# A hybrid decoder block in one kernel: the second feed-forward matmul adds products up in PSUM and scales its results, and the first stage loads x first and ada_w in groups

## The chip, the cores and the metric

The kernel runs on one core of one Trainium2 chip. The metric is the device time of one execution in microseconds (us). Every array lies in HBM at the start and at the end. The engines named below are PE (TensorE), DVE (VectorE), ACT (ScalarE), POOL (GpSimd) and SP (SyncE, which here only issues DMA transfers).

## What is computed

One layer of a decoder for a sequence of 1024 tokens with 1024 features, all in float32. The mixing half of the layer is not touched by the change, so it is left out here:

```python
c_act = jax.nn.silu(c)
mod = (c_act @ ada_w + ada_b)[:, None, :]
sh1, sc1, gt1, sh2, sc2, gt2 = jnp.split(mod, 6, axis=-1)

h = rms_norm(x, norm_mix_g) * (1.0 + sc1) + sh1
p = h @ w_in
...
h = rms_norm(x, norm_ffn_g) * (1.0 + sc2) + sh2
x = x + gt2 * (jnp.square(jax.nn.relu(h @ ffn_w1)) @ ffn_w2)
return rms_norm(x, final_g)
```

`ada_w` is 1024 x 6144, `w_in` is 1024 wide on its contracted side, `ffn_w1` is 1024 x 4096 and `ffn_w2` 4096 x 1024.

## The kernel before, in words

**Precision.** A float32 factor is split in two parts, a rounded high part and the rest, by `split` (L72 an ACT cast, L73 a DVE subtraction). One product of two 128-row tiles is then three matmuls into the same PSUM tile, `mm3` (L112, L113, L114): high with high, high with low, low with high.

**Order.** A scheduler sets the order on each engine from the order in which the code issues its instructions and from a model of their cost; an engine works its queue off in that order, and an instruction that waits holds up what stands behind it. SP's queue holds nearly all loads and stores.

**First stage, `start` (L356 to L437).** The 1024 features are 8 tiles of 128 (`kt`). For each `kt`, `ada_load` fetches the 128 columns of `ada_w` for the shift and the 128 for the scale; `ada_sum` multiplies them by silu(c) and adds them up over the 8 row tiles on DVE (L270 once, L272 seven times, 128x256 each); `ada_col` has PE add over the partitions (L141) and writes the columns `sh` and `s` (L281, L282). The scaled x (L353) is transposed on PE (L338); ACT applies `sh` and `s` and writes the high part `hh` and an exact copy `ev` (L390); `hl`, the low part, is the difference on POOL (L392; for the last `kt` on DVE). `w_load` and `w_split` bring in 384 columns of one row tile of `w_in` as `raw`, `whi`, `wlo`, with two buffers each. `main` then does the matmuls for one `kt` and one half of 512 tokens: 3 column blocks times 3. The loop does half 0 of a `kt` and then half 1 of the one before. The next stage (columns of branch D, `n` and `hh` in the trace) mixes into the end.

**Second feed-forward matmul, `ffn_down` (L1455 to L1625), the last stage.** It multiplies the squared relu, transposed and stored by the stage before in the DRAM array `FA`, by `ffn_w2`. It is one level of a seven-product (Strassen-like) scheme: tokens, contracted features and output columns are each halved, and seven products of sums and differences of blocks take the place of eight. `FA` holds the seven left factors ready-made; the right factors are made here, tile by tile, by `operand`: on POOL (L1498 and L1501, differences of halves of `e` and `o`, which are even and odd row tiles of the weights), then split by ACT and DVE. The contracted side is worked through in two passes `c` of `m` = 8 tiles each; in each pass the seven products `k` run in the tuple `order`, each over 8 tiles (steps) for 4 token tiles `t`, so that one product is 8 x 4 x 3 = 96 matmuls into four PSUM banks. Two sets of four banks (`mm`, and `ch`, `ch`, `ax`, `ax`) take turns.

The gate `gt2` scales columns. Before, it is applied to the weights: in pass 0 inside `operand` (L1495, 24 tiles on DVE, 8 on POOL), and on POOL behind the loads for pass 1 (L1477, 32). `evict` takes each product out of PSUM: in pass 0 into 28 tiles of SBUF (ACT), in pass 1 by a DVE add (L1508); a list `todo` of further DVE adds from SBUF to SBUF combines the products. `lower`, `right` and `top` add x, take the squares for the final norm, and store. The evictions of the stage before, the first feed-forward matmul, are L1406.

## Time and profile before

| | us |
|---|---|
| median of 3 runs | 1723.52 (1723.36 to 1727.23) |
| the profiled execution's own time | 1722.87 |
| its span in the trace | 1721.1 |

The trace has the start and the length of every instruction on every engine in this one execution, and for a wait the instruction that ended it. PE is busy for 95% of the span. Spacing between starts of matmuls is a surer measure of PE than its busy time, because a matmul's record overlaps the next one's; the columns of the windows also give TensorE's granted clock, where 1.00 stands for its upper level of 2.4 GHz and 0.50 for the lower of 1.2 GHz. Times of day below are us from the span's start: the first stage lies at 0 to 93, `ffn_down`'s matmuls at 1372 to 1713.

### The profile page before, as it was taken

To read this page: it belongs to the slowest core of one execution; us is meant where nothing else is said; L and a number is where in the kernel's file an instruction comes from. 1 tells how busy PE (TensorE), PEld (TensorE's weight loads), DVE (VectorE), ACT (ScalarE), POOL (GpSimd) and SP (SyncE) were. 2 spreads that over 40 slices of the span, in tenths; PEclk is the share of its full clock that TensorE was granted. 3 is DMA by queue.
4 is the path that set the end of the run, shared out by engine and by line. 5 is a ranking of instruction groups with operands and counts; after the bars stand their busy time and mean duration, and the time that the engine had idled before them with its cause. 6 is when DMAs were issued, how large, how long until landed. Compare 5 with 4: busy or idle time off the path is not lost.

```text
span 1721.1 us, 22750 instructions
## 1 busy us (share of the span) xinstructions
PE 1626.4 (95%) x8083; PEld 1302.1 (76%) x8083; DVE 1066.9 (62%) x1778; ACT 657.1 (38%) x1214; POOL 688.3 (40%) x536
## 2 busy tenths in 40 slices
PE   4899999999999999999999997899999979999987
PEld 2698777777776877777888775688888757888876
DVE  5674546666539734333444659765555599889986
ACT  4522124555522112121222335544445435544443
POOL 2450223112211222222001457576665486676553
PEclk9999999999999999999999999899999989999998
DMA  8433136777666435332212544454444653563252
GB/s 251 113 99 58 57 118 195 179 187 180 151 124 193 90 112 167 110 96 56 67 44 86 187 142 123 129 184 141 153 153 153 208 189 111 185 194 104 90 180 91
DMA packets 268804, 234.68 MB, mean 136 GB/s; under 512 B 79287, under 2 KB 200362, under 8 KB 268690
## 3 DMA queue, kind: packets, MB, share of 16 engines
q1 hardware_dynamic: 260082, 224.83, 44.1%
q10 hardware_dynamic: 8464, 8.01, 1.9%
q8 instruction: 64, 1.05, 0.3%
q0 software_dynamic: 144, 0.39, 0.1%
q14 instruction: 50, 0.41, 0.1%
HBM read 172.59 MB, written 60.58 MB: 135 GB/s over the span
## 4 chain that ended last, share of the span: by engine, by line
PE 41%; DVE 7%; issue 2%; DMA 1%; POOL 1%; ACT 1%; POOLq 0%; DVEq 0%; SPq 0%; ACTq 0%
PE pmm L113 8%; PE pmm L112 8%; PE pmm L114 8%; PE pax L114 3%; PE pax L113 3%; PE pax L112 3%; PE pch L113 3%; PE pch L114 3%; PE pch L112 3%; DVE g L73 1%; DVE w L1495 1%; DMA raw<-in_ffn_w_dram 1%; DVE xx L73 1%; DMA x<-X 1%; POOL x L1535 0%
## 5 line engine op out<-in xcount | busy, mean ns | idle before, releaser
L112 PE MATMUL pmm<-hh,whi 128*128 128x512 f32 x704 | 287.0, 410 | 2.7 <-ACT hh L390 2.6
L113 PE MATMUL pmm<-hl,whi 128*128 128x512 f32 x704 | 279.5, 397 | 5.5 <-POOL hl L392 5.5
L114 PE MATMUL pmm<-hh,wlo 128*128 128x512 f32 x704 | 279.3, 397 | 3.5 <-DVE wlo L73 3.2
L73 DVE TENSOR_TENSOR wlo<-raw,whi 128x512 fp32r<-128x512 f32 (+1 forms) x140 | 107.2, 802 | 136.4 <-ACT whi L72 133.1
L114 PEld LDWEIGHTS pmm<-hh,wlo 128*128 128x128 f32 x704 | 133.5, 190 | 35.2 <-DVE wlo L73 4.9
L113 PEld LDWEIGHTS pmm<-hl,whi 128*128 128x128 f32 x704 | 134.0, 190 | 34.0 <-POOL hl L392 8.1
L112 PEld LDWEIGHTS pmm<-hh,whi 128*128 128x128 f32 x704 | 133.3, 190 | 33.7 <-ACT hh L390 4.1
L72 ACT CAST whi<-raw 128x512 fp32r<-128x512 f32 (+1 forms) x140 | 79.3, 612 | 159.6 <-PE pmm L113 106.6
L1220 POOL TENSOR_TENSOR m<-m,sig 128x512 f32<-128x512 f32 x32 | 45.1, 1409 | 130.0 <-DVE sig L1217 129.8
L84 POOL TENSOR_TENSOR raw<-raw,gt 128x1024 f32<-128x1024 f32 x16 | 38.8, 2427 | 136.5 <-DMA raw<-in_w_o_dram 131.3
L1203 ACT ACTIVATE sig<-pmm 128x512 f32<-128x512 f32 x64 | 38.1, 595 | 142.7 <-PE pmm L114 135.1
L73 DVE TENSOR_TENSOR g<-raw,g 128x512 fp32r<-128x512 f32 x75 | 79.8, 1064 | 20.1 <-ACT g L72 14.1
L72 ACT CAST g<-raw 128x512 fp32r<-128x512 f32 x75 | 46.5, 619 | 82.1 <-PE pmm L113 47.9
L73 DVE TENSOR_TENSOR g<-w,g 128x512 fp32r<-128x512 f32 x65 | 74.4, 1145 | 3.0 <-ACT g L72 2.8
L1217 DVE TENSOR_TENSOR sig<-pmm,sig 128x512 f32<-128x512 f32 x48 | 33.0, 687 | 68.6 <-PE pmm L114 68.6
L73 DVE TENSOR_TENSOR n<-xx,m 128x512 fp32r<-128x512 f32 x64 | 55.0, 865 | 28.3 <-ACT m L72 28.3
L1501 POOL TENSOR_TENSOR w<-w,w 128x512 f32<-128x512 f32 x32 | 54.4, 1705 | 44.7 <-DVE g L73 34.2
L72 ACT CAST m<-xx 128x512 fp32r<-128x512 f32 x64 | 39.3, 620 | 75.4 <-PE pch L113 27.4
L113 PE MATMUL pmm<-g,g 128*128 128x512 f32 x152 | 61.2, 402 | 6.3 <-DVE g L73 6.3
L112 PE MATMUL pmm<-n,wyh 128*128 128x512 f32 x160 | 66.3, 416 | 0.8 <-ACT n L72 0.8
L1406 DVE TENSOR_TENSOR xx<-pmm,xx 128x512 f32<-128x512 f32 x52 | 35.8, 689 | 47.4 <-PE pmm L114 43.4
L113 PE MATMUL pmm<-n,wyh 128*128 128x512 f32 x160 | 64.6, 404 | 0.0
(522 smaller groups left out, 4383.5 us busy)
## 6 DMA issues: line engine op xcount, KB each, us to landing
raw<-FA SPq DMA_DIRECT2D x56, 512.0 KB
raw<-in_w_in_dram SPq DMA_DIRECT2D x52, 512.0 KB
FA<-xx SPq DMA_DIRECT2D x80, 256.0 KB
raw<-in_ffn_w_dram SPq DMA_DIRECT2D x36, 512.0 KB
mod<-in_ada_w_dram SPq DMA_DIRECT2D x64, 256.0 KB
w<-in_ffn_w_dram SPq DMA_DIRECT2D x32, 512.0 KB
ada<-in_ada_w_dram SPq DMA_DIRECT2D x16, 512.0 KB
raw<-in_w_o_dram SPq DMA_DIRECT2D x16, 512.0 KB
```

The lines of the kernel that those rows point to most:

```text
L72: a = nc.scalar.copy(hi, src)
L73: b = (eng or nc.vector).tensor_tensor(lo, src, hi.bitcast(F32), op=ALU.subtract)
L84: nc.gpsimd.tensor_tensor(raw, raw, scale, op=ALU.mult)
L112: mm(ps, lhsT=lh, rhs=rh, start=start, stop=False)
L113: mm(ps, lhsT=lh, rhs=rl, start=False, stop=False)
L114: mm(ps, lhsT=ll, rhs=rh, start=False, stop=stop)
L1203: nc.scalar.activation(sg, pg, AF.Sigmoid)
L1217: v.tensor_tensor(m if first else sg, py[0], sg, op=ALU.mult)
L1220: nc.gpsimd.tensor_tensor(m, m, sg, op=ALU.add)
L1406: v.tensor_tensor(dst, pts[i, k], u, op=ALU.add)
L1495: eng.tensor_tensor(w[:, h], w[:, h], gt2[:, h], op=ALU.mult)
L1501: gp.tensor_tensor(src, {5: e[:, h1], 6: o[:, h1], 4: o[:, h0]}[k], src, op=ALU.subtract)
```

## The change

**In `ffn_down`.** The order of the products becomes 1, 5, 6, 3, 7, 4, 2. Products 6 and 7 go on adding in the four banks where product 1 stands, and 3 in those of product 5 (`behind`); the banks are read out after 1, 5, 3, 7, 4 and 2, each time with the running sum (`into`). In pass 0 this leaves 16 copies on ACT and 16 adds on DVE; in pass 1, 32 adds from PSUM on DVE, and the adds from SBUF to SBUF are gone but for four in pass 0. The gate scales the results: 8 tiles on DVE and 8 on POOL, and for product 2 of pass 1, whose result goes straight into x, the 8 weight tiles on POOL. x comes in earlier for the upper token tiles, and `lower` runs during the last product, together with `lower_right`.

**In `start`.** x of the first half is loaded ahead of `ada_w`; `ada_w` comes in groups of 1, 1, 2, 2, 2 tiles, where a row of a pair is 1 KB instead of 512 B, and a pair is added up by 8 DVE instructions of 128x512; `w_in` comes in pairs, so that its two buffers hold four tiles; x of the first half is scaled for its first 512 features on ACT; `hl` of half 0 is made on DVE instead of POOL.

The diff, cut to this:

```diff
-    def ada_load(self, j):
+    def ada_load(self, j, n):
...
+        w = self.ADA.tile([P, KT, 2, n * P], F32, tag=f"ada{n}", name=f"ada_{self.n}")
+        src = self.a["ada_w"][0].rearrange("(k p) f -> p k f", p=P)
+        for k in (slice(0, KT // 2), slice(KT // 2, KT)):
+            for sec in range(2):
+                c0 = sec * D + j * P
+                self.nc.sync.dma_start(w[:, k, sec], src[:, k, c0 : c0 + n * P])
...
+                if first and hf == 0:
+                    nc.scalar.activation(x[hf], x[hf], AF.Identity, scale=st[:, 3, t : t + 1])
...
-            eng = v if kt == KT - 1 else nc.gpsimd
+            eng = v if kt == KT - 1 or half == 0 else nc.gpsimd
...
             if kt == 0:
-                with self.tc.issue_after(self.last.ins):
-                    acc.append(self.ada_sum(ada[2]))
-            elif kt + 2 < KT:
-                acc.append(self.ada_sum(ada[kt + 2]))
+                add(2)
+            elif kt in (1, 2):
+                add(3, KT // 2)
+            elif kt in (3, 4):
+                if kt == 3:
+                    ada(6, 2)
+                    w_load(3)
+                add(4, KT // 2)
...
-        order = (1, 7, 5, 6, 4, 3, 2)
+        order = (1, 5, 6, 3, 7, 4, 2)
...
-            if i >= m:
-                for h in (h0, h1):
-                    gp.tensor_tensor(w[:, h], w[:, h], gt2[:, h], op=ALU.mult)
...
-            for eng, w, h in {1: ((v, e, h0), (v, e, h1)), 7: ((v, o, h1),), 5: ((gp, o, h0),)}.get(k, ()):
-                if i < m:
-                    eng.tensor_tensor(w[:, h], w[:, h], gt2[:, h], op=ALU.mult)
+            if k == 2 and i >= m:
+
+                gp.tensor_tensor(o[:, h0], o[:, h0], gt2[:, h0], op=ALU.mult)
...
+        into = {1: ("11",), 5: ("22",), 6: ("12",), 3: ("12",), 7: ("21", "22"), 4: ("21",), 2: ("11",)}
+        behind = {6: 1, 7: 6, 3: 5}
+        ends = (3, 7, 4, 2)
...
+            for j in into[k]:
+                if (j, t) in acc:
+                    a = acc[j, t]
+
+                    add(a, acc["21", t] if c == 0 and j == "22" else pt, a)
+                else:
+                    a = acc[j, t] = self.g()
+                    nc.scalar.copy(a, pt)
+            if c == 1:
+                later = {
+                    1: lambda: join(gp, t, 0, acc["11", t]),
+                    3: lambda: right(t),
+                    7: lambda: scale(gp, acc["22", t], 1),
+                    4: lambda: (lower_right(t), lower(t)),
+                }
...
+                if k in behind:
+                    pts = banks[c, behind[k]]
+                else:
+                    first = (k in (1, 2)) == (c == 0)
+                    pts = [self.ps(tag) for tag in (("mm",) * 4 if first else ("ch", "ch", "ax", "ax"))]
```

The instruction order between the first stage and `ffn_down` is the same on every engine. Three places where it differs:

SP's queue in the first stage, behind the loads of the first two tiles of `ada_w` (`ada`) and of both halves of x. Before, with `raw` a single row tile of `w_in`:

```order
L261 DMA ada_248<-in_ada_w_dram 128x8x128 x2
L365 DMA raw_251<-in_w_in_dram 128x384
L261 DMA ada_253<-in_ada_w_dram 128x8x128 x2
L365 DMA raw_256<-in_w_in_dram 128x384
L261 DMA ada_327<-in_ada_w_dram 128x8x128 x2
L261 DMA ada_390<-in_ada_w_dram 128x8x128
L365 DMA raw_330<-in_w_in_dram 128x384
```

and after the change, with two tiles to each load:

```order
L264 DMA ada_184<-in_ada_w_dram 128x4x256 x4
L374 DMA raw_189<-in_w_in_dram 128x2x384
L264 DMA ada_191<-in_ada_w_dram 128x4x256 x4
L374 DMA raw_196<-in_w_in_dram 128x2x384
L264 DMA ada_481<-in_ada_w_dram 128x4x256 x4
L374 DMA raw_486<-in_w_in_dram 128x2x384
```

What stood there as single tiles of `ada_w` and single row tiles of `w_in` in turn now comes in pairs: three loads of `ada_w`, of four transfers each, bring its tiles 2 to 7, and each has the matching pair of `w_in` behind it. `ada_481` takes over the buffer of `ada_184`, as `raw_330` took over that of `raw_251`.

DVE in the first stage, around the sums for the third tile of `ada_w` (`aacc_318` before, with `aacc_381` that of the fourth; `aacc_322` after the change is that of both). Before:

```order
L272 SCALAR_TENSOR_TENSOR aacc_318<-ada_248,cact,aacc_318 128x256
L270 TENSOR_SCALAR aacc_381<-ada_253,cact 128x256
L272 SCALAR_TENSOR_TENSOR aacc_318<-ada_248,cact,aacc_318 128x256
L272 SCALAR_TENSOR_TENSOR aacc_381<-ada_253,cact,aacc_381 128x256
L272 SCALAR_TENSOR_TENSOR aacc_318<-ada_248,cact,aacc_318 128x256
L73 TENSOR_TENSOR wlo_356<-raw_251,whi_355 128x384
L272 SCALAR_TENSOR_TENSOR aacc_318<-ada_248,cact,aacc_318 128x256
L272 SCALAR_TENSOR_TENSOR aacc_381<-ada_253,cact,aacc_381 128x256
L281 TENSOR_TENSOR sh_95<-pax_341,prmT 128x1
L282 SCALAR_TENSOR_TENSOR s_94<-pax_341,b_122,prmT 128x1
```

after the change, with `m` a tile of x and `wlo` the low part of `w_in`:

```order
L361 TENSOR_SCALAR m_181<-m_181,st_49_289 128x512
L277 SCALAR_TENSOR_TENSOR aacc_322<-ada_184,cact,aacc_322 128x512
L73 TENSOR_TENSOR wlo_355<-raw_189,whi_354 128x384
L277 SCALAR_TENSOR_TENSOR aacc_322<-ada_184,cact,aacc_322 128x512
L73 TENSOR_TENSOR wlo_355<-raw_189,whi_354 128x384
L277 SCALAR_TENSOR_TENSOR aacc_322<-ada_184,cact,aacc_322 128x512 x2
L275 TENSOR_SCALAR aacc_380<-ada_191,cact 128x512
L286 TENSOR_TENSOR sh_95<-pax_340,prmT 128x1
L287 SCALAR_TENSOR_TENSOR s_94<-pax_340,b_122,prmT 128x1
```

The sum of the fourth tile is no longer a row of its own behind the third's shift and scale (`sh`, `s`): both tiles' sums end ahead of them.

DVE where `ffn_down` begins, with `w` the tiles of `ffn_w2`, `gt` the gate, `g` and `xx` split factors. Before:

```order
L1406 TENSOR_TENSOR xx_11795<-pmm_11838,xx_11795 128x512
L73 TENSOR_TENSOR xx_11914<-raw_11873,xx_11913 128x512
L1495 TENSOR_TENSOR w_2052_11883<-w_2052_11883,gt_11866 128x512
L73 TENSOR_TENSOR xx_11916<-w_2051_11881,xx_11915 128x512
L73 TENSOR_TENSOR g_2072_11926<-w_2052_11883,g_2071_11925 128x512
L1495 TENSOR_TENSOR w_2053_11885<-w_2053_11885,gt_11866 128x512
L73 TENSOR_TENSOR g_2087_11956<-raw_11875,g_2086_11955 128x512
L1495 TENSOR_TENSOR w_2053_11885<-w_2053_11885,gt_11866 128x512
L73 TENSOR_TENSOR g_2089_11958<-w_2053_11885,g_2088_11957 128x512
L73 TENSOR_TENSOR xx_11978<-raw_11875,xx_11977 128x512
L1495 TENSOR_TENSOR w_2054_11887<-w_2054_11887,gt_11866 128x512 x2
L73 TENSOR_TENSOR g_2096_12002<-raw_11953,g_2095_12001 128x512
```

after the change, where L1425 is the eviction that was L1406:

```order
L73 TENSOR_TENSOR g_2060_11876<-raw_11831,g_2059_11875 128x512
L1425 TENSOR_TENSOR xx_11775<-pch_11761,xx_11706 128x512
L73 TENSOR_TENSOR g_2062_11878<-w_2042_11841,g_2061_11877 128x512
L73 TENSOR_TENSOR g_2077_11906<-raw_11833,g_2076_11905 128x512
L1425 TENSOR_TENSOR xx_11755<-pax_11779,xx_11755 128x512
L73 TENSOR_TENSOR g_2079_11908<-w_2043_11843,g_2078_11907 128x512
L1425 TENSOR_TENSOR xx_11753<-pmm_11796,xx_11753 128x512
L73 TENSOR_TENSOR xx_11868<-raw_11831,xx_11867 128x512
L73 TENSOR_TENSOR xx_11870<-w_2041_11839,xx_11869 128x512
L73 TENSOR_TENSOR xx_11926<-raw_11833,xx_11925 128x512
L73 TENSOR_TENSOR xx_11928<-w_2044_11845,xx_11927 128x512
L73 TENSOR_TENSOR g_2086_11948<-raw_11903,g_2085_11947 128x512
```

The multiplications by the gate are gone from between the splits, and nothing stands in their place.

## Rows read from the trace of the kernel before

**Rows 1.** The page: PE's busy tenths in 40 slices of 43 us

```profile
PE   4899999999999999999999997899999979999987
```

**Rows 2.** Windows of the first stage: each engine's busy us, clock, DMA share, GB/s

```profile
35.00:40.00 5.00, 1.54 (x5) 1.25 (x5) 2.29 (x7) 0.00 (x0) 3.41 (x1) 0.72 0.27 64
40.00:45.00 5.00, 3.70 (x15) 2.92 (x14) 2.61 (x8) 0.85 (x2) 0.00 (x0) 0.50 0.33 92
...
50.00:55.00 5.00, 5.00 (x30) 4.02 (x28) 4.96 (x13) 3.19 (x5) 2.74 (x2) 1.00 0.83 219
```

**Rows 3.** PE's waits, 0 to 90 us: total, times, longest

```profile
PE pax L141 <- DVE aacc L272: 9.7, 2, 8.4
PE pmm L113 <- POOL hl L392: 5.5, 4, 3.5
```

**Rows 4.** Timeline of DVE and SP: start, length, what, idle time before

```profile
30.74 1.68 DVE L353 TENSOR_SCALAR m<-m,st 128x512 f32<-128x512 f32 x4 [1.14 <-POOL st L350]
...
41.59 0.56 DVE L73 TENSOR_TENSOR wlo<-raw,whi 128x384 fp32r<-128x384 f32 x1 [4.30 <-ACT whi L72]
...
42.17 0.34 SPq L365 DMA_DIRECT2D raw<-in_w_in_dram  x1
...
43.71 0.16 DVE L281 TENSOR_TENSOR sh<-pax,prmT 128x1 f32<-128x1 f32 x1 [0.77 <-PE pax L141]
```

**Rows 5.** Groups of instructions by line, 0 to 90 us: busy, mean ns, idle before

```profile
L392 POOL TENSOR_TENSOR hl<-ev,hh 128x512 fp32r<-128x512 f32 x14 | 21.9, 1571 | 39.0 <-ACT ev L390 39.0
...
L392 DVE TENSOR_TENSOR hl<-ev,hh 128x512 fp32r<-128x512 f32 x2 | 1.4, 692 | 0.6 <-ACT ev L390 0.6
```

**Rows 6.** Timeline of PE at the end of the first stage

```profile
86.25 0.51 PE L112 MATMUL pmm<-n,hh 128*128 128x256 f32 x1
...
91.17 0.40 PE L113 MATMUL pmm<-hl,whi 128*128 128x512 f32 x1
```

**Rows 7.** Timeline of PE in `ffn_down`: first matmuls, first wait, later matmuls, last one

```profile
1372.38 0.39 PE L112 MATMUL pmm<-g,g 128*128 128x512 f32 x1
...
1377.17 0.50 PE L112 MATMUL pmm<-g,g 128*128 128x512 f32 x1 [2.59 <-DVE xx L1406]
...
1379.48 0.63 PE L114 MATMUL pmm<-g,g 128*128 128x512 f32 x1
1379.91 0.63 PE L112 MATMUL pmm<-g,g 128*128 128x512 f32 x1
...
1712.79 0.39 PE L114 MATMUL pax<-g,g 128*128 128x512 f32 x1
```

**Rows 8.** Windows of `ffn_down`, columns as in rows 2

```profile
1410.00:1420.00 10.00, 6.93 (x24) 5.21 (x24) 10.00 (x7) 5.55 (x11) 9.34 (x6) 0.84 0.00 0
...
1450.00:1500.00 50.00, 50.00 (x222) 41.38 (x221) 42.84 (x37) 24.61 (x44) 35.67 (x23) 1.00 0.54 177
```

**Rows 9.** PE's waits, 1340 to 1480 us: first and last of five groups

```profile
PE pch L113 <- DVE g L73: 4.8, 1, 4.8
...
PE pmm L113 <- DVE xx L73: 1.2, 1, 1.2
```

**Rows 10.** PE's waits, 1480 to 1722 us: first and last of three groups

```profile
PE pmm L113 <- DVE xx L73: 4.1, 1, 4.1
...
PE pch L113 <- DVE xx L73: 0.9, 1, 0.9
```

**Rows 11.** Groups of instructions by line, 1370 to 1450 us

```profile
L1495 DVE TENSOR_TENSOR w<-w,gt 128x512 f32<-128x512 f32 x22 | 30.3, 1402 | 0.0
...
L1495 POOL TENSOR_TENSOR w<-w,gt 128x512 f32<-128x512 f32 x8 | 13.8, 1729 | 0.0
...
L1501 POOL TENSOR_TENSOR w<-w,w 128x512 f32<-128x512 f32 x8 | 13.4, 1675 | 8.0 <-DVE g L73 4.3 <-DVE xx L73 3.7
```

**Rows 12.** Groups by line, 1480 to 1722 us

```profile
L1508 DVE TENSOR_TENSOR n<-n,m 128x512 f32<-128x512 f32 x16 | 16.1, 1024 | 0.0
...
L1527 DVE SCALAR_TENSOR_TENSOR x<-x,st,fg 128x512 f32<-128x512 f32 x12 | 8.6, 750 | 5.2 <-POOL st L1522 5.2
```

More of the change, by code (lines that the diff above doesn't have):

```diff
@@ L377, in start, with add @@
         self.new_h()
-        ada = [self.ada_load(0)]
+        raws, ws, accs = [], [], []
+        sums = []
+        ada = lambda j, n: sums.append(self.ada_sum(self.ada_load(j, n), n, accs))
         xs = [self.load_x(0)]
-        raws = [w_load(0), w_load(1)]
-        ada.append(self.ada_load(1))
+        ada(0, 1)
+        w_load(0)
+        ada(1, 1)
         xs.append(self.load_x(1))
+        ada(2, 2)
+        w_load(1)
+        ada(4, 2)
+        w_load(2)
         pts = [self.ps(t) for t in ("mm", "mm", "mm", "mm", "ch", "ch")]
+        def add(g, n=KT):
+            for _ in range(n):
+                next(sums[g], None)
         def pre(kt, half):
@@ L1525, in normed, with join @@
         def normed(tt, ch, r):
-            x = x1[tt][:, ch]
+            x = x1[tt, ch]
             v.scalar_tensor_tensor(x, x, r, fg[:, ch], op0=ALU.mult, op1=ALU.mult)
         def put(tt, ch):
-            nc.sync.dma_start(self.out[0, tt * P : tt * P + P, h1 if ch else h0], x1[tt][:, ch])
+            nc.sync.dma_start(self.out[0, tt * P : tt * P + P, h1 if ch else h0], x1[tt, ch])
+        def join(eng, tt, ch, a):
+            scale(eng, a, ch)
+            gp.tensor_tensor(x1[tt, ch], x1[tt, ch], a, op=ALU.add)
         def lower(t):
             tt = 4 + t
-            for ch in range(2):
-                gp.tensor_tensor(x1[tt][:, ch], x1[tt][:, ch], acc[4 + ch, t], op=ALU.add)
-                square(tt, ch, acc[4 + ch, t])
+            join(v, tt, 0, acc["21", t])
+            square(tt, 0, acc["21", t])
             r = root(tt)
@@ L1590, in ffn_down @@
             b_load(i, 1)
-        x1 = {}
+        banks = {}
         for s, (c, k, i) in enumerate(steps):
@@ L1604, in ffn_down @@
                     tok = slice(t * P, t * P + P)
-                    self.mm3(pts[t], ah[:, tok], al[:, tok], bh, bl, q == 0, q == m - 1)
+                    self.mm3(pts[t], ah[:, tok], al[:, tok], bh, bl, q == 0 and k not in behind, q == m - 1 and k in ends,
+                             open_=True)
                     if q == m - 1:
```

130 lines of the change are left out of this document (58 added, 72 removed).

## The prediction

> **What bounds the kernel now.** I read the page's slices first. PE is at nine tenths or more in most of them [rows 1]; the dips are slices 1 and 2 (0 to 86 us), 25 and 26 (1033 to 1119), 33 (1377 to 1420) and the last two (from 1635). At 25 and 26 no engine's order changes, so nothing there can move; the others lie in the two stages that the change touches. That leaves two places.
>
> The first is 35 to 50 us. PE does 1.54 of 5 us, then 3.70, and the 3.70 at the lower clock, 0.50 [rows 2]. The waits name what PE stands for: 9.7 us on the sums of `ada_w` (one wait of 8.4), and 5.5 us on `hl` from POOL [rows 3]. DVE's timeline shows why the sum is late. DVE itself stands idle for 4.30 us until 41.59, because the next row in its queue splits a tile of `w_in`, and the rest of the sum stands behind that row; the shift of the third tile then comes at 43.71 [rows 4]. The DMA engines are as idle as PE there (share 0.27, 64 GB/s [rows 2]), since SP's next load waits for that same buffer and goes out at 42.17 [rows 4]. So buffers and the order on DVE bound this stretch, not bytes. From 50 us PE works without a gap, and one `kt` (30 instructions of PE) takes 5.0 us [rows 2].
>
> The second is `ffn_down`. From the first matmul at 1372.38 to the end of the last, 1713.2, are 340.8 us [rows 7]. An undisturbed stretch has 220 whole matmuls in 50.00 us (222 with those cut by its edges [rows 8]), 0.227 us each. There are 2 x 7 x 96 = 1344 matmuls, so 305.5 us would do, and **35.3 us are lost**. Early, up to 1430, five groups of waits make 15.6 us (4.8, 4.2 in two, 2.8, 2.6 and 1.2; their first and last are [rows 9]), and behind them some 36 matmuls run 0.43 us apart instead of 0.227 (1379.48 to 1379.91 [rows 7]), 7.2 us more: about 23. The other 12 lie after 1650: three waits of 7.1 us, the first and last 4.1 and 0.9 [rows 10], and the slow matmuls behind them. All waits but one name DVE's splits, and DVE is busy for 10.00 of 10 us early on [rows 8].
>
> **The change, part by part.**
>
> *Gate, early half.* DVE loses 24 multiplications L1495; in 1370 to 1450 there are 22 of them, 30.3 us [rows 11]. POOL loses 8 of 1.73, 13.8 us [rows 11]. The splits' inputs do not wait for anything new: weights are used as they land. DVE's queue was 23 us behind PE at most and gets 30.3 us shorter, so these stalls should nearly all go. Two things can keep some. POOL must still make the differences for the second product, 1.68 us each [rows 11], now earlier, because 5 is second and not 7; and the loads of `FA` for that product stand on SP behind the stage before's stores and eight loads of `o`. I keep one wait like the smaller ones of rows 9 and its slow matmuls: 1.2 + 9 x 0.2 = 3 us. Bounds: 0, and half of the 23 if POOL becomes the maker that is waited for. Gain 20, between 11 and 23.
>
> *Order and accumulation, late half.* The matmuls are the same 1344. Evictions in pass 0: 12 ACT copies go, and 16 DVE adds of about 0.69 come, 11 us in a pass of 160 us in which DVE has over 7 free in 50 (42.84 of 50.00 [rows 8]) even before L1495 is gone: hidden. In pass 1, 24 adds from PSUM become 32 (8 x 0.69 = 5.5 us more), and the adds from SBUF to SBUF go, 16 of them alone 16.1 us [rows 12]. Eight scalings come on DVE, at 0.7 to 1.4 each [rows 11], 6 to 11 us. So DVE has from about 0 to 5 us less there, but POOL is rid of 32 multiplications and gets 24 back (8 scalings, 8 weights, 8 joins), and DVE's operations are shorter when POOL is silent: L1495's mean is 1.40 us against 0.69 for a like operation in the first stage [rows 5, 11]. What is late next is the end: `lower` now runs inside the last product. Each of its four rounds needs a scaling on DVE, a join on POOL, a square on ACT, the root on POOL, and then two scalings by the root on DVE (0.75 each [rows 12]), and three splits of the last product stand on DVE between those rounds. Adding the rounds up, the last split is ready some 15 us into the last product and wanted after 13; 2 us, and 5 of the matmuls behind it slow, 1 us. Bounds: 0 and the longest wait of rows 10, 4.1, with 9 slow ones, 6. Gain 12 - 3 = 9, between 6 and 12.
>
> For the banks: a rule stands against this change. A bank is read out by one engine while PE wants to add to it again, and the trace has such a wait, 2.59 us at 1377.17 on an eviction [rows 7]. The Trainium skill (PSUM — Partial Sum Buffer, "PSUM bank collisions raise a hardware error") says that two engines must not touch one bank in the same cycle, so PE has to be held while a running sum is read; the row agrees, and this is the slower rival below. I cost it at nothing, because the other four banks hold a whole product meanwhile, 96 x 0.227 = 21.8 us.
>
> `ffn_down` together: 20 + 9 = **29 us**, between 17 and 35.
>
> *First stage.* (a) x first: the first matmul can't come much earlier, since both x and the first `ada_w` tile are wanted; 0.5 us, not counted. (b) The pair of sums for tiles 2 and 3. DVE begins on the second half of x at 30.74 as before [rows 4]. Then come 8 rows of x at 0.42 (1.68 for four [rows 4]), 8 sums of 128x512 and two splits. For a sum of 512 I take 0.69, the row of another operation of that size [rows 5]: 30.7 + 3.4 + 5.5 + 1.1 = 40.7, and as the first rows are a little earlier with less of x left to DVE, 40. The split of `w_in` doesn't wait any more, as its pair has a buffer of its own. The shift follows 0.8 later, as now, [rows 4]: 40.8 against 43.71. (c) That sum holds tile 3 too, which had its own wait. So PE goes on without a stop: two `kt` at the lower clock, 8 us each (some 1.6 times the 5.0, as the windows at 0.50 run [rows 2]), then four at 5.0, and 2 us to drain: 40.8 - 1 (tokens of half 1 of tile 1 are still to be done) + 16 + 20 + 2 = 77.8. The same point before: 86.25 to 91.17 belongs to the next stage, and 6 matmuls follow it [rows 6], so 92.6 - 4.9 = 87.7. Gain 10. (d) Later sums: two more pairs, about 8.5 us of DVE each, ready at 49 and 58; wanted by PE at 56 and 66. Covered; uncovered, the last would cost what it is late. (e) `hl` of half 0 on DVE: 8 x 0.69 more on DVE, and the 5.5 us of waits for POOL at 1.57 shrink [rows 3, 5]; contained in (c). (f) New: the small loads for branch D's constants stand on ACT's queue behind the last evictions of this stage, while PE's order has a transpose of them near its old place. If it comes up short, PE waits. No row shows it; the nearest is the longest wait for a neighbour, 3.5 [rows 3]. Between 0 and 3.5 I take 2.
>
> First stage: 10 - 2 = **8 us**, between 3 and 14 (the upper end is both long waits of rows 3 gone without any half-speed behind them).
>
> **Sum.** The profiled execution took 1722.87, which is 0.65 below the median of 1723.52: the same within the noise. 1722.87 - 29 - 8 = 1685.9, so **1686 us**.
>
> **Rivals.**
>
> *The first stage gives nothing.* The wait moves to (f) or to the last pair, whose load waits until the first pair's sum is done. For: three things there are new. Against: DMA engines idle at 0.27 there. 1722.9 - 29 = 1694.
>
> *Half of the early stalls stay*, with POOL as the maker that is waited for: it was busy for 9.34 of 10 us [rows 8], and its differences for product 5 come sooner. 1686 + 11 = 1697. Against: 13.8 us of POOL's own work goes.
>
> *Both places come out clean*: 35 and 12 to 14 gained, 1722.9 - 48 = 1675.
>
> *Slower: the banks.* If PE has to stand at each change of product for the eviction of the banks it needs next, each costs the 2.6 us of rows 7 and nine slow matmuls, 4.4 us. With 13 changes 57 us: 1686 + 57 = 1743. It decides from the ninth change on (37 / 4.4 = 8.4). Against: 21.8 us lie between an eviction and the next use, while four DVE adds take 2.8 us; only a DVE queue 19 us behind would do it.
>
> *The change moves nothing that is waited for.* Loads of `FA` and weights bound `ffn_down`, and the waits only change their name. Against: DMA share 0.00 in the worst window [rows 8]. About 1722.
>
> **How the numbers follow.** Chances: forecast (1680 to 1691) 0.50, first stage gives nothing 0.13, half of the early stalls 0.15, both clean 0.15, nothing moves 0.03, banks 0.04. A measurement of this kernel can tell 0.3%, 5 us, from no change; so faster 0.93, same 0.03, slower 0.04. The range takes in the forecast, the two weaker cases and the clean one: 1675 to 1699, which leaves less than 2 in 10 outside with what each estimate may miss.
>
> **What would show it.** In the trace after: no wait of PE above 3 us for a sum of `ada_w`, the first stage's matmuls done near 78; no DVE window at 10.00 of 10 in 1390 to 1430 (old times); PE's waits for splits early in `ffn_down` under 4 us in all, and 20 to 30 us less from its first matmul to its last. The forecast is wrong if PE waits for POOL's differences in the second product, if the wait for a transpose near the end of the first stage is above 3.5 us, or if the last product shows a gap of more than 4 us behind `lower`; and wrong altogether if waits for evictions stand at every change of product.

## The result, and the profile after

The changed kernel takes 1697.99 us (median of 4 runs, 1696.88 to 1699.67), the kernel before 1723.48 in the runs beside it. The ratio is 0.9848, 95% interval [0.9831, 0.9865]: 1.5% faster, 25.5 us, where 37 were forecast. The time lies in the range, near its slow end, and at the two rivals that were priced at 1694 and 1697, but for neither of their reasons. The profiled execution took 1698.43 (span 1696.7), against 1722.87 (1721.1).

Where its 24.4 us came from shows in PE's timeline: the end of the first stage, the first matmuls of `ffn_down`, and its last product with the last matmuls.

```profile
87.76 0.40 PE L112 MATMUL pch<-hh,wlo 128*128 128x512 f32 x1
...
1369.24 2.21 PE L112 MATMUL pmm<-g,g 128*128 128x512 f32 x9
1372.06 2.11 PE L112 MATMUL pmm<-g,g 128*128 128x512 f32 x8 [0.61 <-DVE xx L1425]
...
1658.89 1.53 PE L112 MATMUL pch<-xx,xx 128*128 128x512 f32 x6
...
1672.87 0.50 PE L112 MATMUL pch<-g,g 128*128 128x512 f32 x1 [0.85 <-ACT g L72]
1677.95 3.78 PE L112 MATMUL pch<-g,g 128*128 128x512 f32 x8 [4.57 <-DVE g L73]
...
1688.52 0.85 PE L112 MATMUL pax<-g,g 128*128 128x512 f32 x3
```

`ffn_down` starts 3.1 us sooner (1372.38 in rows 7), runs 320.1 us from its first matmul to the end of its last instead of 340.8 (20.7 less), and behind its last matmul 7.3 us follow instead of 7.9: 3.1 + 20.7 + 0.6 = 24.4.

Since PE's four banks change name from product to product, the timeline also gives the length of each product. An undisturbed one takes 21.8 us in every trace (96 x 0.227). What the 14 products take above that, by pass (the 12 matmuls of the stage before that share the first banks, 2.8 us, taken off):

| `ffn_down`, us lost | pass 0 | pass 1 | together |
|---|---|---|---|
| before | 24.1 | 11.2 | 35.3 |
| after | 4.1 | 10.5 | 14.6 |
| forecast for after | 3 | 3 | 6 |

So the early half did what was forecast, 20.0 us, and the late half nothing, 0.7. PE's waits after the change, first of 1320 to 1460 us (they answer to rows 9), then of 1460 to 1697 (rows 10):

```profile
PE pch L112 <- DVE g L73: 1.1, 2, 0.7
PE pmm L112 <- DVE xx L1425: 0.6, 1, 0.6
PE pch L112 <- ACT g L72: 0.5, 1, 0.5
PE pmm L112 <- DVE xx L73: 0.3, 1, 0.3
...
PE pch L112 <- DVE g L73: 4.6, 1, 4.6
PE pch L112 <- DVE st L1536: 1.6, 1, 1.6
PE pch L112 <- ACT g L72: 0.9, 1, 0.9
```

15.6 us of early waits have become 2.5. Late there were 7.1 and still are, but at another place: before, 9.7 of the 11.2 us were lost in product 3; now 8.7 of 10.5 are lost in the very last product, which takes 30.5 us (1658.89 to 1689.37).

The windows of the first stage answer to rows 2, the last one to rows 8:

```profile
35.00:40.00 5.00, 0.96 (x3) 0.49 (x3) 5.00 (x9) 1.86 (x4) 3.88 (x1) 0.79 0.65 213
40.00:45.00 5.00, 4.55 (x17) 3.85 (x18) 4.17 (x8) 0.05 (x1) 0.39 (x1) 0.53 0.17 44
45.00:50.00 5.00, 4.20 (x24) 3.14 (x22) 4.86 (x6) 2.74 (x4) 1.29 (x1) 1.00 1.06 357
...
1410.00:1420.00 10.00, 10.00 (x46) 8.20 (x45) 10.00 (x9) 5.19 (x10) 7.48 (x6) 1.00 0.73 233
```

In the first stage PE still stands between 35 and 40 us, now with the DMA engines busy (0.65) and DVE at 5.00 of 5. In 1410 to 1420 DVE is still at 10.00 of 10, a sign that the prediction had wanted gone, and yet PE works through 46 matmuls at the upper level, 1.00: what counts is whether DVE is behind, and it isn't.

### The profile page after: what moved, and what is told of

The parts are those of the page before. It is cut to its first block, busy times and chain, and to the rows that moved or that the text cites. A ratio compares the mean times of both kernels' runs of the same rounds, so it can differ in the third digit from the quotient of the medians.

```text
span 1696.7 us, 22664 instructions
## 1 busy us (share of the span) xinstructions
PE 1613.8 (95%) x8083; PEld 1293.7 (76%) x8083; DVE 1004.0 (59%) x1729; ACT 652.4 (38%) x1206; POOL 631.0 (37%) x505
## 4 chain that ended last, share of the span: by engine, by line
PE 37%; DVE 8%; DMA 2%; issue 2%; ACT 2%; POOL 1%; POOLq 0%; DVEq 0%; ACTq 0%; SPq 0%
PE pmm L112 22%; PE pax L112 8%; PE pch L112 7%; DVE g L73 2%; DVE xx L73 1%; DMA raw<-in_ffn_w_dram 1%; DVE m L1523 1%; DMA raw<-FA 1%; DMA w<-in_ffn_w_dram 1%; ACT g L72 1%; DVE wlo L73 0%; POOL ev L1513 0%; DVE m L1526 0%; DVE m L1328 0%; DVE n L73 0%
## 5 line engine op out<-in xcount | busy, mean ns | idle before, releaser
L72 ACT CAST whi<-raw 128x512 fp32r<-128x512 f32 (+1 forms) x140 | 79.0, 612 | 158.2 <-PE pmm L112 141.5
L112 PE MATMUL pmm<-g,g 128*128 128x512 f32 x456 | 107.3, 390 | 0.6 <-DVE xx L1425 0.6
L112 PE MATMUL pmm<-n,wyh 128*128 128x512 f32 x320 | 106.3, 411 | 0.8 <-ACT n L72 0.8
L73 DVE TENSOR_TENSOR g<-raw,g 128x512 fp32r<-128x512 f32 x75 | 72.0, 959 | 48.7 <-ACT g L72 42.6
L112 PEld LDWEIGHTS pmm<-g,g 128*128 128x128 f32 x456 | 85.6, 188 | 18.9 <-DVE xx L1425 1.0
L112 PE MATMUL pmm<-g,m 128*128 128x512 f32 x256 | 82.5, 404 | 3.4 <-ACT m L72 3.4
L72 ACT CAST g<-raw 128x512 fp32r<-128x512 f32 x75 | 46.5, 620 | 69.8 <-PE pmm L112 34.6
L112 PEld LDWEIGHTS pmm<-n,wyh 128*128 128x128 f32 x320 | 60.5, 193 | 16.4 <-issue 1.2
L72 ACT CAST m<-xx 128x512 fp32r<-128x512 f32 x64 | 39.3, 620 | 75.8 <-PE pch L112 27.4
L112 PE MATMUL pch<-g,g 128*128 128x512 f32 x222 | 59.7, 402 | 8.7 <-DVE g L73 5.7
```

The lines of the kernel that those rows point to most:

```text
L72: a = nc.scalar.copy(hi, src)
L73: b = (eng or nc.vector).tensor_tensor(lo, src, hi.bitcast(F32), op=ALU.subtract)
L112: mm = lambda *x, **y: self.nc.tensor.matmul(*x, **y, skip_group_check=open_)
```

## Experiments: the parts of the change

**`ffn_down` alone.** Order, accumulation and gate as in the change, first stage as before.

> The first stage of the kernel before with the changed second feed-forward matmul. By the trace after, its matmuls take 320.1 us from first to last where they took 340.8, and the end behind the last is 0.6 us shorter. If the two parts don't touch each other, this kernel is 21 us faster than before: 1702 to 1703 us. The rival is that the shorter first stage changes what the DMA queues hold later; then this kernel differs from 1702 by more than 3 us.

Measured: 1703.15 us, ratio 0.988 [0.9866, 0.9895]: 1.2%, 20.7 us. Its products lose 3.3 us in pass 0 and 10.9 in pass 1, as in the whole change.

**`start` alone.**

> The changed first stage with the second feed-forward matmul of before. By the two traces the first matmul of the last stage comes 3.1 us earlier (1369.2 against 1372.4), so 1720 us. The prediction's own figure for this part was 8 us, 1715. Below 1716 would say that the changed last stage hides part of the gain; 1723 or more that the 3 us came from elsewhere.

Measured: 1718.14 us, ratio 0.9966 [0.9955, 0.9978]: 5.9 us, between 3.8 and 7.8. The parts multiply to 0.988 x 0.9966 = 0.9846, and the whole gave 0.9848: within these intervals the two don't touch each other. The 5.9 us are more than the 3.1 that were expected of this part and less than the prediction's 8.

**The gate alone.** Products in the old order and the old evictions; only the multiplications move from the weights to the results.

```diff
-            if i >= m:
-                for h in (h0, h1):
-                    gp.tensor_tensor(w[:, h], w[:, h], gt2[:, h], op=ALU.mult)
...
-                if i < m:
-                    eng.tensor_tensor(w[:, h], w[:, h], gt2[:, h], op=ALU.mult)
+            if k == 2 and i >= m:
+                gp.tensor_tensor(o[:, h0], o[:, h0], gt2[:, h0], op=ALU.mult)
...
+                scale(gp if ch else v, acc[4 + ch, t], ch)
```

> The kernel before with one thing changed: the gate scales the results instead of the weights (8 tiles on DVE, 8 on POOL, 8 weight tiles on POOL for the last product); the order of the products, the 28 copies and the adds from SBUF to SBUF stay. Theory: the early stalls, 23 us, come from the 24 multiplications on DVE, so nearly all of the gain of the last stage is here: 1700 to 1706 us, with PE's waits for splits before 1430 below 4 us. Rival: the stalls come from the order of the products and the evictions; then 1717 or more.

Measured: 1720.89 us, ratio 0.9982 [0.9973, 0.9991], 3 us, where some 20 were expected. Pass 0 loses 2.0 us instead of 24.1, so the gate by itself is the whole of the early term, and the rival, which gave these stalls to the order of the products, is out. But pass 1 loses 30.3 instead of 11.2. PE's waits from 1480 us on:

```profile
PE pch L113 <- DVE g L73: 6.4, 3, 3.5
PE pmm L113 <- DVE xx L73: 3.8, 2, 2.2
PE pmm L113 <- DVE g L73: 3.6, 3, 1.6
PE pch L112 <- ACT g L72: 1.9, 2, 1.6
...
```

and groups of DVE in it between 1550 and 1720 us (line, engine, operation, count, busy us, mean ns):

```profile
L1504 DVE TENSOR_TENSOR n<-n,m 128x512 f32<-128x512 f32 x16 | 17.3, 1093 | 0.0
L1504 DVE TENSOR_TENSOR m<-m,m 128x512 f32<-128x512 f32 x12 | 13.6, 1134 | 0.0
...
L1508 DVE TENSOR_TENSOR n<-n,gt 128x512 f32<-128x512 f32 x8 | 5.3, 681 | 0.0
```

The kernel before has the same additions from SBUF to SBUF there, at 1024 and 680 ns (16.1 and 8.2 us), and DVE was busy for 95.12 of the 100 us from 1550 to 1650 with PE whole. Eight scalings more (5.3 us) and slower additions (another 6.6 in these two groups) find no room in that. Of the 17.6 us that PE waits there, 13.8 name DVE's splits and 3.8 ACT's casts.

**Order and accumulation alone**, the gate still on the weights.

```diff
-        order = (1, 7, 5, 6, 4, 3, 2)
+        order = (1, 5, 6, 3, 7, 4, 2)
...
-            for eng, w, h in {1: ((v, e, h0), (v, e, h1)), 7: ((v, o, h1),), 5: ((gp, o, h0),)}.get(k, ()):
+            for eng, w, h in {1: ((v, e, h0), (v, e, h1)), 5: ((v, o, h1), (gp, o, h0))}.get(k, ()):
...
+        def scale(eng, a, ch):
+            pass
```

> The kernel before with the new order and the adding up in PSUM alone; the gate scales the weights as before (24 tiles on DVE and 8 on POOL in the first pass, 32 on POOL in the second). Theory: DVE's queue at the start of the last stage is as long as before, so the early stalls stay, 20 us or more, and the late ones change by some us either way: 1717 to 1727. Rival (order and adding up are what helps): below 1710.

Measured: 1722.14 us, ratio 0.9987 [0.9974, 1.0]: no difference that can be told. Pass 0 loses 24.0 (the longest wait 8.9 on a split), pass 1 8.6.

What follows from these two: the parts of `ffn_down` are not a sum. The gate alone gives 3 us, order and accumulation alone 2 (an interval that reaches to nothing), and both together 21. By passes, the gate alone saves 22.1 us and costs 19.1; order and accumulation alone save 0.1 and 2.6. The gate moves DVE's and POOL's work from the start of the stage to its end, and there the other part makes room for it. That it does so by taking the additions from SBUF to SBUF away fits DVE's rows above, but no run parts the accumulation from the new order.

## Experiments: the last product

**Without `lower`.** The first theory for the 8.7 us was that the rows of `lower` stand on DVE ahead of the last splits. This kernel leaves out the scaling, the join, the squares, the root and the norm of the lower four tiles.

```diff
-            join(v, tt, 0, acc["21", t])
-            square(tt, 0, acc["21", t])
-            r = root(tt)
...
-                normed(tt, ch, r)
...
-            square(4 + t, 1, acc["22", t])
```

> The changed kernel without the joining and the norm of the lower four token tiles (they are stored as they were loaded, with no scaling, join, square, root or product with the root), so that nothing of that stands on DVE between the splits of the last product. The output of these tiles is therefore not the reference's. Theory: the 4.6 us wait, the 0.9 us wait and the slow matmuls behind them, 8.7 us in the last product of the trace after, come from this chain alone: 1689 to 1690 us, and the last product takes 22 us. Rival: the splits come late because of their casts, loads or buffers; then 1696 or more.

Measured: 1692.14 us, ratio 0.9809 [0.9791, 0.9826], some 2 us above the expected time. The last product takes 22.0 us: 8.4 us of the loss are gone, and pass 1 loses 2.1 in all. So the rows of `lower` are the cause, and not casts, loads or buffers by themselves. DVE's timeline in the changed kernel shows how:

```profile
1667.76 1.41 DVE L1546 SCALAR_TENSOR_TENSOR x<-x,st,fg 128x512 f32<-128x512 f32 x2
...
1669.20 0.68 DVE L1526 TENSOR_TENSOR m<-m,gt 128x512 f32<-128x512 f32 x1
1670.34 2.44 DVE L1546 SCALAR_TENSOR_TENSOR x<-x,st,fg 128x512 f32<-128x512 f32 x2 [0.45 <-POOL st L1541]
1672.69 0.68 DVE L1526 TENSOR_TENSOR m<-m,gt 128x512 f32<-128x512 f32 x1
...
1673.42 0.68 DVE L73 TENSOR_TENSOR g<-raw,g 128x512 fp32r<-128x512 f32 x1
1675.76 1.42 DVE L1546 SCALAR_TENSOR_TENSOR x<-x,st,fg 128x512 f32<-128x512 f32 x2 [1.66 <-POOL st L1541]
...
1677.21 0.68 DVE L73 TENSOR_TENSOR g<-w,g 128x512 fp32r<-128x512 f32 x1
```

The scaling L1526 of the third tile of `lower` (1669.20) stands behind the norm L1546 of the first, that of the fourth (1672.69) behind the norm of the second. Each round therefore begins only when an older one has come back from POOL's join, ACT's square and POOL's root; in between DVE waits (1.66 us for `st`) with the last split, at 1677.21, queued behind it. PE took that split up 0.74 us later, at 1677.95. ACT's queue does the same on a smaller scale: the cast L72 at 1672.22, which ends PE's wait of 0.85 us at 1672.87, stands behind a square that waits for POOL's join:

```profile
1671.59 0.63 ACT L1534 ACTIVATE m<-x 128x512 f32<-128x512 f32 x1 [3.22 <-POOL x L1554]
```

**`lower`'s rows out of the way.** Scalings directly behind the additions that make their input; root, norm and store issued two tiles at a time behind steps 4 and 5 of the last product.

```diff
-            join(v, tt, 0, acc["21", t])
+            gp.tensor_tensor(x1[tt, 0], x1[tt, 0], acc["21", t], op=ALU.add)
             square(tt, 0, acc["21", t])
+
+        def lower_out(t):
+            tt = 4 + t
             r = root(tt)
...
+            if c == 1 and k == 4:
+                scale(v, acc["21", t], 0)
...
+            if c == 1 and k == 2 and q in (4, 5):
+                for t in (0, 1) if q == 4 else (2, 3):
+                    lower_out(t)
```

> The changed kernel with the chain of the lower tiles taken apart: the four scalings stand right behind the four adds of that product, and root, product with the root and store are issued behind the splits of the last steps. All work stays. Theory (DVE stands for POOL and ACT inside the chain while splits wait behind it): most of the 8.7 us goes, 1690 to 1693 us. Rival (the work itself is too much for DVE and POOL there, not its order): 1696 or more.

Measured: the last product takes 23.5 us, 7.0 less than in the changed kernel, with all of the work still there: it is the order of the rows that costs PE its time. But the time is 1696.74 us, ratio 0.9839 [0.9823, 0.9855]: 1 us less, not to be told from the changed kernel's and above the 1690 to 1693 expected. Most of PE's gain was given back behind PE: 12.1 us follow its last matmul, where 7.3 did. DVE's timeline there:

```profile
1676.52 2.74 DVE L1546 SCALAR_TENSOR_TENSOR x<-x,st,fg 128x512 f32<-128x512 f32 x4 [0.54 <-POOL st L1541]
1679.17 0.68 DVE L1523 TENSOR_TENSOR n<-pch,n 128x512 f32<-128x512 f32 x1
...
1682.19 0.68 DVE L1523 TENSOR_TENSOR n<-pch,n 128x512 f32<-128x512 f32 x1
...
1685.21 0.68 DVE L1523 TENSOR_TENSOR n<-pax,n 128x512 f32<-128x512 f32 x1
...
1688.22 0.68 DVE L1523 TENSOR_TENSOR n<-pax,n 128x512 f32<-128x512 f32 x1
```

The four `top` tiles follow each other 3.02 us apart: addition, square on ACT, L1540, root on POOL, L1546, and only then the next addition. PE needs 2.73 us for a tile (12 x 0.227), so once the first addition is late, nothing catches up. Here it came at 1679.17, behind four rows L1546 (2.74 us); the last one begins at 1688.22, 5.3 us after PE's last matmul (1682.89).

**Half of the norm moved to POOL and ACT** ("tail"), to clear those rows:

```diff
+            normed(tt, 0, r)
+            put(tt, 0)
+            nc.scalar.activation(x, x, AF.Identity, scale=r)
+            put(tt, 1)
...
+            gp.tensor_tensor(x1[4 + t, 1], x1[4 + t, 1], fg[:, 1], op=ALU.mult)
```

> The changed kernel with the chain of the lower tiles taken off the way of both its neighbours: scalings and joins of the left halves on DVE directly behind the adds, the product with final_g of the right halves on POOL one product earlier and their product with the root on ACT, roots behind the last splits. In the run with the chain only re-ordered PE's matmuls of the last stage took 312.8 us instead of 320.1, but the time fell by 1.3 us only, because the first add of the last results then came 2.4 us late on DVE behind products with the root, and four serial rounds of 3.0 us set the end. Theory: with DVE free there the end follows PE by 7 us again, 1690 to 1692 us. Rival: the four rounds bind anyway; then 1695 or more.

Measured: 1695.38 us, ratio 0.9834 [0.9811, 0.9857], not to be told from the changed kernel's. That is the rival's time. `ffn_down` lasts 316.2 us in its trace, 3.9 less than in the changed kernel, and 9.3 us follow it, 2.0 more. A new wait of PE stands at the end of product 4; it is shown with ACT's square and DVE's splits ahead of it:

```profile
PE pmm L112 <- DVE g L73: 2.6, 1, 2.6
...
1654.01 0.63 ACT L1534 ACTIVATE m<-x 128x512 f32<-128x512 f32 x1 [1.89 <-POOL x L1570]
...
1655.28 1.76 DVE L73 TENSOR_TENSOR g<-raw,g 128x512 fp32r<-128x512 f32 x1 [5.06 <-ACT g L72]
1656.96 1.77 DVE L73 TENSOR_TENSOR xx<-w,xx 128x512 fp32r<-128x512 f32 x1
```

Two things make it. POOL has four multiplications more among its joins, so ACT's squares, which wait for the joins, come later, and the casts behind them too: DVE stands idle for 5.06 us. And then, beside a busy POOL, three splits take 1.75 to 1.77 us instead of 0.68, 3.2 us more than they need alone. No run tells the two apart; the work that was moved off DVE came back through both. **The same with the first stage of ada_first** (below):

> Both edits in one: the chain of the lower tiles out of the way, and the first tile of ada_w loaded ahead of x. They lie at the two ends of the kernel and should add up: 2 us less than the run with the first edit alone, 1688 to 1690 us, if that run comes out as expected there. If their gains overlap, it is within 1 us of that run.

Measured: 1697.19 us, ratio 0.9837 [0.9817, 0.9856], with the same wait of 2.6 us. The gain that was expected of the pair didn't come.

## Experiments: the first stage

**`ada_w` first.** x of half 0 is loaded behind the first tile of `ada_w` again; all else as in the change.

```diff
-        xs = [self.load_x(0)]
         raws, ws, accs = [], [], []
...
+        xs = [self.load_x(0)]
```

> The changed kernel with one line moved back: the first tile of ada_w is loaded ahead of x of the first half. In the trace after, that tile lands at 13.8 us (8.0 before) and the first matmul comes at 22.1 (19.1 before). Theory: x first costs the first stage some 2 us all along, because the second tile's sum and with it the second half of x and the sum of the pair come later: 1695.5 to 1696.5 us, with the first matmul near 19. Rival: the pair's sum is bound by x of the second half, not by the first tile; then 1698, no change.

Measured: 1696.03 us, ratio 0.9837 [0.9818, 0.9856]; 2 us less than the changed kernel, inside the intervals. In its trace the first matmul of `main` comes at 20.44 instead of 22.11 (near 19 was expected), the shift of the third tile at 42.88 instead of 44.05. DVE's timeline of the changed kernel holds what it undoes:

```profile
13.76 0.35 DVE L275 TENSOR_SCALAR aacc<-ada,cact 128x256 f32<-128x256 f32 x1 [9.50 <-DMA ada<-in_ada_w_dram]
...
32.50 1.67 DVE L361 TENSOR_SCALAR m<-m,st 128x512 f32<-128x512 f32 x4 [1.13 <-POOL st L355]
...
39.19 1.74 DVE L277 SCALAR_TENSOR_TENSOR aacc<-ada,cact,aacc 128x512 f32<-128x512 f32 x1
...
44.05 0.16 DVE L286 TENSOR_TENSOR sh<-pax,prmT 128x1 f32<-128x1 f32 x1 [0.80 <-PE pax L142]
```

With x ahead, the first tile of `ada_w` is there at 13.76 (before: 7.95). Everything behind it slides, the scaling of the second half of x too (32.50 against 30.74 in rows 4).

**`hl` of the first `kt` on DVE**, half 1 too, because PE's longest wait beside the sums is for POOL's `hl`, 4.1 us, the one long operation in the 3.88 us that POOL is busy in 35 to 40:

```diff
-            eng = v if kt == KT - 1 or half == 0 else nc.gpsimd
+            eng = v if kt in (0, KT - 1) or half == 0 else nc.gpsimd
```

> The changed kernel with the low part of the first tile for half 1 on DVE too. On POOL it took 4.27 us in the trace after (36.1 to 40.4), beside a DVE that was never idle, and PE waited 4.05 us for it. Theory: this wait and its six slow matmuls are worth 3 us, and the pair's sum, whose instructions took up to 1.7 us beside POOL instead of 0.7, ends earlier: 1694 to 1696 us. Rival: PE would have waited for the pair's sum anyway, which ends at 42.9; then within 1 us of 1698.

Measured: 1698.32 us, ratio 0.985 [0.983, 0.987], as the rival had it. The wait for `hl` is gone, that for the sums has grown, and the stage's last matmul comes at 90.37, where five traces with the first stage of the change have 86.04 to 88.23. The first row is the changed kernel's (waits, 0 to 90 us); behind it are this kernel's waits, its second wait for a sum in PE's timeline, and a window:

```profile
PE pax L142 <- DVE aacc L277: 15.6, 1, 15.6
```

```profile
PE pax L142 <- DVE aacc L277: 19.6, 2, 16.3
...
43.91 0.98 PE L142 MATMUL pax<-ones,aacc 128*128 128x1 f32 x4 [3.26 <-DVE aacc L277]
...
45.00:50.00 5.00, 4.98 (x18) 4.11 (x18) 3.94 (x9) 2.78 (x4) 1.26 (x1) 0.50 1.02 337
```

The waits of 15.6 and 16.3 us are those for the first tile, ahead of the first matmul, and have nothing to do with this edit. New is the one of 3.26 us, for the pair: PE waits for the pair's sum anyway, and the wait for `hl` only lies inside it. The shift of the third tile comes 0.9 us later than in the changed kernel, the stage's end 2.6, and the rest goes with the clock: from 45 to 50 us PE works without a gap at 0.50, where the changed kernel has 1.00.

**Third and fourth tile summed up singly**, so that the third's shift need not wait for the fourth:

```diff
-        ada(2, 2)
+        ada(2, 1)
...
+        ada(3, 1)
...
+                add(3)
```

> The changed kernel with the sums and loads of tiles 2 and 3 of ada_w one by one again (tiles 4 to 7 stay in pairs). Theory: the pair's sum makes the third tile wait for the fourth: its shift came at 44.05 us in the trace after, and would come at 40 to 41; worth 1 to 3 us: 1695 to 1697. Rival: what PE gains at the third tile it waits for at the fourth, whose sum then ends at 43 or later: within 1 us of 1698.

Measured: 1697.48 us, ratio 0.9844 [0.9824, 0.9864], no difference that can be told. The shift of the third tile comes at 41.24 instead of 44.05, the stage's last matmul at 85.21 instead of 87.76, but `ffn_down` begins at 1369.44, where it did (1369.24). The unchanged stages between vary by more than that: from the start of the first stage's last matmul to `ffn_down`'s first, the 14 traces of this study have 1278.3 to 1285.1 us. So the first stage is better read at its own end. With the old one its last matmul stands at 92.20 to 92.93 in four traces (mean 92.6), with that of the change at 86.04 to 88.23 in five (87.4), with `ada_w` first at 85.95 to 86.55 in three (86.2): the change gives 5.2 us there, `ada_w` first 1.2 more. Whether all of it arrives is open: the stages between took 1280.4 us in the mean of the four and 1282.2 in that of the five. Whether single sums are worth the 2 us that the trace shows can't be told from these runs.

## Experiment: the two lessons together

`ada_w` first; scalings behind their additions; the join on DVE; and root, norm and store one tile at a time, behind steps 4 and 5 and the last two behind step 7, with nothing moved to POOL.

```diff
+                for t in {4: (0,), 5: (1,), 7: (2, 3)}.get(q, ()):
+                    lower_out(t)
```

> The changed kernel with three edits: in the first stage x of half 0 is again loaded behind the first tile of ada_w and its later groups as in ada_first; in the last product of ffn_down the scalings of lower's sums stand right behind the adds that make them and the join with x is a DVE add; and the root, the two scalings by it and the stores of lower's four tiles are issued one at a time behind the last splits (the first after step 4, the second after step 5, the last two after step 7), with nothing more moved to POOL. Theory (the late loss is the rows of lower on DVE that stand ahead of the last splits; what is left then is the chain of the four top tiles): no wait of PE above 2 us for a split in the last product, first to last matmul of ffn_down near 312 as in split_lower, the first add of top 1 to 2 us late behind rows of lower, four rounds of 3.0 us behind it; with about 2 us from the first stage as in ada_first, 1691 to 1694. Rival (the end is bound by DVE's sum of rows wherever they stand): PE's wait goes, but the first add of top comes 3 us or more late, and the time is 1695 to 1697, that of ada_first or split_lower.

Measured: 1693.65 us (5 runs), ratio 0.9818 [0.9804, 0.9831]: 4.3 us less than the changed kernel, whose interval it just touches at 0.9831. The last product takes 22.0 us, pass 1 loses 2.2, and `ffn_down` takes 311.8 from its first matmul to its end. `ffn_down` begins at 1369.42, no sooner than in the changed kernel, so in this trace the 4.4 us between the spans (1696.7 and 1692.3) are all from its end. DVE's timeline there:

```profile
1673.15 3.40 DVE L1546 SCALAR_TENSOR_TENSOR x<-x,st,fg 128x512 f32<-128x512 f32 x5 [0.42 <-POOL st L1541]
1676.47 0.68 DVE L1523 TENSOR_TENSOR n<-pch,n 128x512 f32<-128x512 f32 x1
...
1687.86 0.75 DVE L1546 SCALAR_TENSOR_TENSOR n<-n,st,fg 128x512 f32<-128x512 f32 x1 [0.66 <-POOL st L1541]
```

PE is through at 1681.2 and the last norm begins at 1687.86: the four rounds bound the end, and the first of them still stands behind five rows of `lower`, 3.7 us behind its tile (1659.16 + 60 x 0.227 = 1672.8), where 1 to 2 were expected and the rival had 3 or more. Of the 8.3 us that `ffn_down` is shorter, 4.4 reach the end.

## Why the prediction came out as it did

The time lies 12 us above the forecast of 1686, outside the 1680 to 1691 that were given a chance of 0.50, and 1 us inside the range. That it lies inside is owed to the width of the range, which was set to hold the weaker rivals, and not to the sum. Of the signs, two came: early in `ffn_down` all of PE's waits together are 2.5 us, and it takes 20.7 us less from its first matmul to its last. Three did not: the first stage's matmuls end at 88.2 and not near 78, PE waits 15.59 us for a sum of `ada_w`, and DVE has a window at 10.00 of 10. One of the signs of being wrong came too, the gap behind `lower`.

**The loss it began with: right.** It was put at 35.3 us, 23 early and 12 late. Product by product it is 24.1 and 11.2.

**Early term, 20 us: right, and for its reason.** Measured 20.0. The gate alone gives it, the accumulation alone none of it, and POOL did not become the maker that is waited for: no wait in the first 90 us of the stage names it.

**Late term, 9 us: mis-sized, and this is the larger part of the miss (8.3 of some 12 us).** The old late loss did go, as the 12 of the sum said: without `lower` only 2.1 us are left. What failed is the 3 set against it. The sentence that failed is "the last split is ready some 15 us into the last product and wanted after 13". PE wanted it 14.5 us in (1672.87 + 0.50), and had it after 19.1 (1677.95). The rounds had been added up as if each ran as soon as its input was there. In DVE's queue the third and fourth tile's scalings stand behind the first and second tile's norms, so the rounds follow each other; split_lower, with only the order of these rows changed, has 7.0 of the 8.7 us back. The loss, 8.7 us, lies above the bound of 6 too, since that bound was a wait of another kind, one split late and not a chain of four engines. The prediction's own sign for it, a gap above 4 us behind `lower`, is there with 4.57. A second late loss, 1.9 us in product 7, was not in the sum; there POOL is busy without a pause (1619.28 to 1632.82) and DVE's splits take 1.7 us.

**What it had not seen: the two halves of `ffn_down` hang together.** It cost gate and accumulation side by side, 20 and 9. Either alone gives 3 us or less: without the other part, what the gate saves early it costs late.

**The end behind PE: not in the sum.** The four rounds of 3.02 us bound the end as soon as PE is faster: in split_lower 4.8 of the 7.3 us by which `ffn_down` became shorter were lost again behind it, and in best 3.8 of 8.3.

**Banks at nothing: right.** The longest wait for an eviction is 0.61 us, at 1372.06, on the stage before's, and outside the first two products, product 7 of pass 1 and the last one every product takes 21.8. Nowhere is a running sum waited for, so the rule that was set beside it has no price here: an eviction and the next use of its bank lie a product apart. (The banks are read out behind product 6 as well, which the list in the section on the change leaves out: `evict` runs after every product.)

**First stage, 8 us: mis-sized, and begun with a wrong reading.** Of the 9.7 us of waits for sums that were laid to 35 to 50 us, the 8.4 end at 12.00, ahead of the first matmul; in the stretch are 1.30 us, and before them 3.46 for POOL's `hl` and PE at the lower clock. The upper bound of 14, which took the 8.4 as a thing to win there, has no ground either. PE's timeline before, and last the row after the change that answers to the first:

```profile
12.00 1.02 PE L141 MATMUL pax<-ones,aacc 128*128 128x1 f32 x4 [8.37 <-DVE aacc L272]
...
38.46 0.80 PE L113 MATMUL pmm<-hl,whi 128*128 128x512 f32 x1 [3.46 <-POOL hl L392]
...
42.69 0.98 PE L141 MATMUL pax<-ones,aacc 128*128 128x1 f32 x4 [1.30 <-DVE aacc L272]
```

```profile
19.09 1.01 PE L142 MATMUL pax<-ones,aacc 128*128 128x1 f32 x4 [15.59 <-DVE aacc L277]
```

The stage gave 3.1 us in the profiled pair, 5.2 by the mean place of the stage's last matmul, and 5.9 (3.8 to 7.8) by the time of the part alone. Step by step:
- (a) "x first, 0.5 us": of the wrong sign. The first matmul comes at 22.11, before at 19.08. Two things were wanted together, and the change delayed the one that arrives last. ada_first gets 1.7 of the 3.0 back.
- (b) The shift at 40.8: it came at 44.05, before at 43.71. Of the 3.25 us, 1.8 are the later start (32.50), 0.4 are eight sums of 0.74 instead of 0.69, and one of them next to POOL's `hl` took 1.74, another 1.
- (c) The time behind the shift: this is where the gain came from. From the shift to the stage's last matmul it is 43.7 us instead of 48.6; 4.9 us, and 0.3 off for the later shift, is the 4.6 by which the stage ends sooner. The forecast had some 7 here and 2.9 from the shift. Its reason, that one sum holds two tiles, is not the cause: with the third and fourth tile summed up singly the same stretch takes 44.0 us (41.24 to 85.21). What the traces show in its place are two things. Four waits for `wlo`, the low part of `w_in`, 3.2 us in all between 55 and 82 us, are gone in the change, where `w_in` comes in pairs (the row behind this list; after the change there is none). And PE was at the upper level again in 45 to 50 us (1.00, before 0.75), sooner than the two slow `kt` of the forecast. How much each of these gave, no run shows.
- (e) `hl` on DVE: the long wait stayed, since half 1 of the first tile is still made on POOL: 4.05 us at 40.45, where it was 3.46 at 38.46. In 35 to 40 us PE does 0.96 us of work, before 1.54.
- (f) The wait for branch D's constants, 2 us: not there. No wait in the stage names them.

(c) rests on this row of PE's waits before the change, 0 to 90 us:

```profile
PE pmm L114 <- DVE wlo L73: 3.2, 4, 1.3
```

Taken together, 29 + 8 became 20.7 + 3.1, and 0.6 at the end. If the rounds of `lower` had been laid out row by row in the new order of DVE, with the releaser of each, the queue that made the miss would have shown.

## What to carry to other kernels

Work that is taken off a busy stretch has to be followed to where it goes: the gate alone moved 22 us of stalls and got 19 of them back in a later stretch of the same engine. A chain of several engines that runs beside matmuls is costed by the order of its rows on each engine that it shares, not by the sum of its durations, since one row that waits holds every row behind it, splits for PE among them. And when PE gets faster at the end of a program, look at once for the serial rounds behind it: their pitch (here 3.02 us against PE's 2.73) decides what the gain is worth.

## What the runs showed of the hardware that was not expected

- **DVE and POOL slow each other down.** A DVE split of 128x512 takes 0.68 us alone and 1.71 to 1.78 where POOL runs additions or products without a pause; a POOL operation of that size takes 1.28 to 1.30 alone and 1.70 to 1.74 beside DVE's splits. From 1619 to 1632 us in the changed kernel both start at the same pitch of 1.70 us, so they seem to take turns. Not every DVE operation does: the additions L1523 from 1638.70 to 1643.57, which read one input from PSUM, take 0.67 us, and POOL's operations beside them 1.29. The Trainium skill (SBUF — State Buffer, "SBUF: two separate sides") says that a DVE operation with two inputs in SBUF and a POOL operation that reads SBUF hold a port pair as an exclusive lock for the whole instruction. That agrees with which operations slow each other here; the pitch of 1.70 us is less than the 0.68 + 1.28 of two whole records, so these can't be locked out of each other for their whole recorded length. The price here is 1.1 us for each such DVE operation.
- **The row that a wait names need not be its cause.** The 1.62 us in product 7 are put down to `st` L1536 on DVE, but the matmul that waits reads `g`. What ends the wait is the split of `g` directly ahead of that row on DVE (1.76 us beside POOL), which ends as the row begins, 1631.6.
- **Unchanged stages move.** The same instructions between the first stage and `ffn_down` took 1278.3 to 1285.1 us in 14 traces, a spread as large as the first stage's whole gain.
